# Hybrid trunk on one core: the product of a hi weight tile with the hi and lo halves of x becomes one of 512 columns, in strips 256 wide

## The chip, the cores and the metric

The kernel runs on one core of one Trainium2 chip. The metric is the device time of one execution in microseconds (us). The kernel before took 2446.97 us, the median of 3 runs (2446.15 to 2449.27).

## The reference, cut to what matters

One sequence of T = 256 tokens with D = 2048 features goes through two layers in float32. Each layer is a mixer and a dense SwiGLU, both between RMS norms:

```python
x = x + rms_norm(mixer(rms_norm(x, pre)), post)
x = x + rms_norm((silu(h @ w_gate) * (h @ w_up)) @ w_down, ffn_post)   # h = rms_norm(x, ffn_pre)
```

D_FF is 5632, so w_gate and w_up are 2048 x 5632 and w_down is 5632 x 2048. The mixer of the even layer is one input projection (2048 x 4384), an S5 state-space part, an RWKV-7 part and an output projection (2048 x 2048). The mixer of the odd layer is an input projection (2048 x 4096), a causal convolution over 4 tokens, gates from eight 256 x 256 blocks, a linear recurrence, and an output projection (2048 x 2048). All weights are float32 and are read once from memory, some 400 MB.

## The kernel before, in words

**Layout.** Features lie on the 128 partitions, tokens along the free axis. An activation is 16 tiles of 128 x 256 (one per 128 features, called a k tile where it is multiplied). A weight tile of 128 x 128 is the stationary operand, a tile of x the moving one, and the product, 128 output features x 256 tokens, adds up in PSUM over the k tiles.

**Hi and lo halves.** Float32 accuracy is kept with operands of type float32r: each operand z is split into hi, a rounded copy made on ScalarE, and lo = z - hi, made on VectorE (`split`, L288, through the helpers at L136 and L112). A weight tile times a tile of x is three products: hi with xh (L513), hi with xl (L514), lo with xh (L515), each of 256 columns, each with a weight load of its own. The text calls these three a triple.

**The weight stream.** Weights come in groups: one DMA of 512 KB, 2 k tiles by 512 output columns, into a tile `raw`; ScalarE writes `hi`, VectorE writes `lo`, in rings of 3 buffers (4 after the even layer). `plan` (L431) lists all groups in the order of use, `fetch` (L404) starts their DMAs, `ready` (L415) issues their splits three groups ahead of TensorE.

**Strips.** A `Strip` (L460) makes 512 output columns: four tiles of 128 features accumulate side by side in two PSUM banks (`psw0`, `psw1`, two of each), over all k tiles (`run`, L493). At its end (`done`, L535) an evac function reads PSUM: `first_evac` (L1477) copies on ScalarE, `last_evac` (L1483) adds to what lies in SBUF on VectorE, `gate` (L1658) multiplies by 1/rms of each token, applies silu, multiplies gate by up and splits the result into `hhi` and `hlo`. The last strip of a product finishes its PSUM banks one after the other (`tail`, L527).

**Stages.** Even layer: input strips w_u, w_lr and w_p, with S5 and RWKV work of many small float32 products between them, then w_glu and two halves of the output projection w_eo. SwiGLU: two halves, each of 11 gate-and-up strips and 4 down strips over 22 k tiles. Odd layer: 8 strips w_oi (256 columns of the gelu branch and 256 of the recurrent one), each but the first followed by a short strip w_gt of the gate blocks of the block before (2 k tiles), then 4 strips w_oo. Then the second SwiGLU. At the start of a stage `post` (L1579) makes the new x tile by tile, and the first strip follows it.

**Order.** Nothing is reordered at run time within an engine. What runs beside the weight stream is written as generators in lanes (`Lanes`), and the code issues their next step when an estimate of the engines' times says that its input is there. L.now, the estimate of TensorE's time, goes on by 0.327 for each triple. This decides only the order in which instructions stand on each engine.

## Time and profile before

| what | value |
|---|---|
| median of 3 runs | 2446.97 us |
| span of the profiled execution | 2446.8 us |
| TensorE matmul busy | 2373.5 us, 97% of the span |
| TensorE weight load busy | 2328.5 us, 95% |
| VectorE busy | 1469.4 us, 60% |
| ScalarE busy | 1181.0 us, 48% |
| GpSimd busy | 411.8 us, 17% |
| mean granted TensorE clock | 0.983 of full speed |
| read from memory | 397.98 MB, 164 GB/s over the span |

The trace holds one execution; its span from the first to the last instruction is 2446.8 us, so it and the median of the runs agree within 0.2 us. Matmuls are pipelined, and the end of each is modelled: a single one of 256 columns is shown as some 280 ns long, although the next one starts some 120 ns after it. So the length of a product is read here as the distance from its start to the start of the next, or as the length of a stretch divided by the number of products in it, and not as its mean duration. TensorE has two rows: PE for products, PEld for weight loads, which run while the product before streams. In order of time the stages are: even layer to 578 us, first SwiGLU to 1350 us, odd layer to 1663 us, second SwiGLU to the end.

### The profile page before, as it was taken

Reading aid. Unit: us, or ns where it says so; the run is one execution under the profiler, and the core shown is the slowest. Engines: PE = TensorE matmul, PEld = TensorE weight load, DVE = VectorE, ACT = ScalarE, POOL = GpSimd, SP = SyncE. Lnnn points to the kernel's source line nnn. Section 1 sums busy time; section 2 is a strip of 40 time slices with the busy share of each in tenths; the row PEclk is TensorE's granted clock in tenths of the full one; section 3 lists DMA queues with packets and bytes.
Section 4 is the critical chain, followed back from the end, with each engine's and each line's share of the span. In section 5 each row is a group of like instructions: output and inputs, shape, how many; then the busy total and the mean of one; then the engine's idle time right before and its main releaser. Section 6 shows DMA issues by size and latency. Waiting matters only on the chain.

```text
span 2446.8 us, 47370 instructions
## 1 busy us (share of the span) xinstructions
PE 2373.5 (97%) x19830; PEld 2328.5 (95%) x19830; DVE 1469.4 (60%) x2002; ACT 1181.0 (48%) x1550; POOL 411.8 (17%) x589
## 2 busy tenths in 40 slices
PE   7889999999999999999999999999999999999997
PEld 7888988998999999999999899998999999999997
DVE  8777667558655544555544877757555544555544
ACT  5547555545444434434433588845444444444443
POOL 4753666506000000000000400014000000000002
PEclk8888999999999999999999999999999999999999
DMA  5122543444555555555555455554555555555553
GB/s 198 58 71 73 156 123 113 143 141 164 186 185 182 185 186 184 182 186 183 183 187 181 139 181 188 175 197 138 183 185 186 182 187 183 183 186 183 182 186 116
DMA packets 127446, 404.21 MB, mean 165 GB/s; under 512 B 26112, under 2 KB 26880, under 8 KB 127104
## 3 DMA queue, kind: packets, MB, share of 16 engines
q1 hardware_dynamic: 126912, 399.61, 48.6%
q8 instruction: 155, 2.54, 0.4%
q0 software_dynamic: 320, 1.58, 0.2%
q14 instruction: 59, 0.48, 0.1%
HBM read 397.98 MB, written 3.15 MB: 164 GB/s over the span
## 4 chain that ended last, share of the span: by engine, by line
PE 73%; DVE 3%; POOL 1%; ACT 1%; issue 1%; POOLq 0%; ACTq 0%; DVEq 0%
PE psw L513 24%; PE psw L515 24%; PE psw L514 24%; DVE lo L112 1%; DVE xl L131 1%; POOL xr L112 1%; ACT hi L136 0%; PE ssq L263 0%; PE warm L263 0%; PE own L515 0%; PE own L514 0%; PE own L513 0%; POOL sqs L112 0%; DVE sqs L112 0%; POOL tg L112 0%
## 5 line engine op out<-in xcount | busy, mean ns | idle before, releaser
L112 DVE TENSOR_TENSOR lo<-raw,hi 128x1024 fp32r<-128x1024 f32 (+1 forms) x760 | 930.8, 1229 | 864.8 <-ACT hi L136 860.5
L136 ACT ACTIVATE hi<-raw 128x1024 fp32r<-128x1024 f32 (+1 forms) x760 | 783.7, 1035 | 938.6 <-PE psw L514 738.4
L514 PE MATMUL psw<-xl,hi 128*128 128x256 f32 x3328 | 942.2, 283 | 15.1 <-DVE xl L131 14.8
L513 PE MATMUL psw<-xh,hi 128*128 128x256 f32 x3328 | 941.4, 283 | 0.9 <-ACT xh L136 0.9
L515 PE MATMUL psw<-xh,lo 128*128 128x256 f32 x3328 | 940.3, 283 | 0.0
L514 PEld LDWEIGHTS psw<-xl,hi 128*128 128x128 f32 x3328 | 635.2, 191 | 19.8 <-DVE xl L131 19.8
L513 PEld LDWEIGHTS psw<-xh,hi 128*128 128x128 f32 x3328 | 635.3, 191 | 1.5 <-ACT xh L136 1.5
L515 PEld LDWEIGHTS psw<-xh,lo 128*128 128x128 f32 x3328 | 635.5, 191 | 0.0
L515 PE MATMUL psw<-hhi,lo 128*128 128x256 f32 x1364 | 384.4, 282 | 0.0
L513 PE MATMUL psw<-hhi,hi 128*128 128x256 f32 x1364 | 384.3, 282 | 0.0
L514 PE MATMUL psw<-hlo,hi 128*128 128x256 f32 x1364 | 383.8, 281 | 0.0
L112 POOL TENSOR_TENSOR sqs<-sqs 128x512 f32<-128x512 f32 x44 | 73.1, 1661 | 1518.8 <-ACT sqs L136 1518.4
L515 PEld LDWEIGHTS psw<-hhi,lo 128*128 128x128 f32 x1364 | 257.7, 189 | 0.0
L514 PEld LDWEIGHTS psw<-hlo,hi 128*128 128x128 f32 x1364 | 257.7, 189 | 0.0
L513 PEld LDWEIGHTS psw<-hhi,hi 128*128 128x128 f32 x1364 | 257.7, 189 | 0.0
L513 PE MATMUL psw<-hh,hi 128*128 128x256 f32 x560 | 175.8, 314 | 2.7 <-ACT hh L136 1.4
L514 PE MATMUL psw<-hl,hi 128*128 128x256 f32 x560 | 165.5, 296 | 5.3 <-DVE hl L131 5.3
L515 PE MATMUL psw<-hh,lo 128*128 128x256 f32 x560 | 165.6, 296 | 4.2 <-DVE lo L112 4.2
L513 PEld LDWEIGHTS psw<-hh,hi 128*128 128x128 f32 x560 | 112.8, 202 | 10.5 <-issue 5.6
L514 PEld LDWEIGHTS psw<-hl,hi 128*128 128x128 f32 x560 | 113.0, 202 | 6.2 <-DVE hl L131 5.9
L515 PEld LDWEIGHTS psw<-hh,lo 128*128 128x128 f32 x560 | 112.6, 201 | 5.8 <-DVE lo L112 5.6
L136 ACT ACTIVATE ga<-ga 128x512 f32<-128x512 f32 x52 | 32.9, 632 | 83.0 <-DVE ga L112 82.9
(426 smaller groups left out, 2760.6 us busy)
## 6 DMA issues: line engine op xcount, KB each, us to landing
raw<-in_w_fg SPq DMA_DIRECT2D x352, 512.0 KB, 3.5
raw<-in_w_fd SPq DMA_DIRECT2D x176, 512.0 KB, 3.5
raw<-in_w_oi SPq DMA_DIRECT2D x64, 512.0 KB, 3.9
raw<-in_w_p SPq DMA_DIRECT2D x64, 384.0 KB, 3.2
raw<-in_w_eo SPq DMA_DIRECT2D x32, 512.0 KB, 3.6
raw<-in_w_oo SPq DMA_DIRECT2D x32, 512.0 KB, 4.1
raw<-in_w_u SPq DMA_DIRECT2D x16, 512.0 KB, 4.0
raw<-in_w_glu SPq DMA_DIRECT2D x8, 512.0 KB, 3.5
```

Source lines behind the costliest of these rows:

```text
L112: e.tensor_tensor(o, x, y, op=op)
L131: e.scalar_tensor_tensor(o, x, s, y, op0=op0, op1=op1)
L136: S.activation(o, x, f, bias=bias, scale=scale)
L513: TE.matmul(o, hi[:, kk, sl], xh, start=st, stop=False, skip_group_check=True)
L514: TE.matmul(o, hi[:, kk, sl], xl, start=False, stop=False, skip_group_check=True)
L515: TE.matmul(o, lo[:, kk, sl], xh, start=False, stop=en, skip_group_check=True)
```

## The change

A tile of x now holds hi and lo next to each other (512 columns, class `Pair`; `hh` and `oh` likewise). One product of hi with both halves has 512 columns and fills one PSUM bank, its first half with hi times xh and its second with hi times xl; the product of lo with xh adds to the first half. A weight tile therefore takes two products and two weight loads instead of three. One output tile now takes a whole bank, so a strip is two tiles wide (256 columns, `W2`) and a group is 4 k tiles by 256 columns, the same 512 KB. The two halves in PSUM are added when they are read: ScalarE copies the second half of both tiles to SBUF, VectorE adds the first (`merged`, into a ring of two tiles `mo`). In `last_evac` VectorE adds both halves to SBUF itself, in two instructions.

What depends on the width moves along. `first_evac`, `gate` and the rest read the merged tile in SBUF. The gate strips of a SwiGLU hold one gate tile and one up tile; its halves are 24 and 20 such strips (`HF`) with 24 and 20 k tiles in the down products, 8 strips each. At a stage's start two strips run side by side (`two`), so that each new tile of x is still used by four output tiles. The odd layer has separate strips for the recurrent branch (`hawk_x`) and the gelu branch (`hawk_g`); the gate strips use four banks of their own (`own`). There ScalarE first writes the second half plus the bias to SBUF, VectorE adds the first half, and then the sigmoid runs over 512 columns; two products of 512 columns go from VectorE to GpSimd. L.now goes on by 0.335 for each pair. The diff, cut to its core:

```diff
+        class Pair:
+            def __init__(self, n, name):
+                self.s = [slot8(name=f"{name}{j}").rearrange("p (k z) t -> p k z t", z=2) for j in range(n // 4)]
...
+            def __call__(self, k):
+                return self.s[k // 4][:, k % 4]
...
-                self.ps = Banks(tail)
+                if own:
+                    self.ps = [bank("own").rearrange("p (z t) -> p z t", z=2) for _ in widths]
+                else:
+                    t = psw.tile([P, 2, 2, T], F32, tag="w", name="psw")
+                    self.ps = [t[:, j] for j in range(2)]
+                    self.both = t
...
-                        TE.matmul(o, hi[:, kk, sl], xh, start=st, stop=False, skip_group_check=True)
-                        TE.matmul(o, hi[:, kk, sl], xl, start=False, stop=False, skip_group_check=True)
-                        TE.matmul(o, lo[:, kk, sl], xh, start=False, stop=en, skip_group_check=True)
-                        L.now += 0.327
+                        TE.matmul(o, hi[:, kk, sl], x, start=k == 0, stop=False, skip_group_check=True)
+                        TE.matmul(o[:, 0], lo[:, kk, sl], x[:, 0], start=False, stop=en, skip_group_check=True)
+                        L.now += 0.335
...
+            def merged(self, o=None):
+                w, n = min(self.widths), len(self.widths)
+                if o is None:
+                    while len(held) > 1:
+                        L.step()
+                    o = mg.tile([P, 2, T], F32, tag="mo", bufs=2, name="mo")[0:w, 0:n]
+                    held.append(self)
+                act(o, self.both[0:w, 0:n, 1], AF.Copy)
+                tt(V, o, self.both[0:w, 0:n, 0], o, ADD)
+                return o
...
+        def two(a, b):
+            for g in range(a.kg - 1):
+                ta, tb = a.take(g), b.take(g)
+                for kk in range(0, a.kc, 2):
+                    for z, t in ((a, ta), (b, tb)):
+                        z.run(*t, kks=(kk, kk + 1))
+            for z in (a, b):
+                z.go(z.kg - 1)
...
             def first_evac(y, s):
-                def f(ps):
-                    for j in range(2):
-                        act(yv(y, s, j), ps[:, 2 * j:2 * j + 2], AF.Copy)
+                def f(z):
+                    z.merged(yv(y, s))
...
+                    if add:
+                        tt(V, o, z.both[:, n, 0], o, ADD)
+                        tt(V, o, z.both[:, n, 1], o, ADD)
+                    else:
+                        act(o, z.both[:, n, 1], AF.Copy)
+                        tt(V, o, z.both[:, n, 0], o, ADD)
...
+        def normed_later(z, rstd, rest):
+            o = z.merged()
+            def f():
+                while "rstd" not in rstd:
+                    yield 0.3
+                yield from after(rstd["rstd"])
+                tt(V, o, o, bc(rstd["rstd"], 1, 2), MUL)
+                yield from after(o)
+                yield from rest(o)
+            return f()
...
                 def gate(i):
+                    def rest(o):
+                        g = o[:, 0]
+                        act(g, g, AF.Silu)
+                        yield from after(g)
+                        tt(V, g, g, o[:, 1], MUL)
+                        yield from after(g)
+                        split(hh[:, i, 0], hh[:, i, 1], g)
+                        have.add(i)
+                    return lambda z: normed_later(z, rstd, rest)
...
             def gates(n):
-                        act(sr[:, j], pg[:, j], AF.Sigmoid, 1.0, vc("br", i))
-                        act(si[:, j], pg[:, 2 + j], AF.Sigmoid, 1.0, vc("bi", i))
+                    for o, q, b in ((sr, 0, "br"), (si, 2, "bi")):
+                        for j in range(2):
+                            act(o[:, j], z.ps[q + j][:, 1], AF.Identity, 1.0, vc(b, 2 * n + j))
+                    for o, q in ((sr, 0), (si, 2)):
+                        for j in range(2):
+                            tt(V, o[:, j], z.ps[q + j][:, 0], o[:, j], ADD)
+                            rel(z.ps[q + j])
...
+                        for o in (sr, si):
+                            yield from after(o)
+                            act(o, o, AF.Sigmoid)
...
-                        tt(V, si, si, xc, MUL)
+                        tt(G, si, si, xc, MUL)
```

On TensorE, in the down products of the SwiGLU, the kernel before issues three products of 256 columns for each of the four output tiles (`hhi` and `hlo` are the halves of the moving operand, `psw0` and `psw1` the two banks):

```order
L513 MATMUL psw1_14691<-hhi_11263,hi_14756 128x256
L514 MATMUL psw1_14691<-hlo_11264,hi_14756 128x256
L515 MATMUL psw1_14691<-hhi_11263,lo_14757 128x256
...
L513 MATMUL psw0_14690<-hhi_11263,hi_14756 128x256
L514 MATMUL psw0_14690<-hlo_11264,hi_14756 128x256
L515 MATMUL psw0_14690<-hhi_11263,lo_14757 128x256
```

The changed kernel issues two there, at the end of one strip and the start of the next:

```order
L515 MATMUL psw_8563<-hh_6075,hi_8611 128x512
L516 MATMUL psw_8563<-hh_6075,lo_8612 128x256
L515 MATMUL psw_8563<-hh_6075,hi_8611 128x512
L516 MATMUL psw_8563<-hh_6075,lo_8612 128x256
L515 MATMUL psw_8703<-hh_6075,hi_8635 128x512
L516 MATMUL psw_8703<-hh_6075,lo_8636 128x256
```

Each weight tile has one product and one weight load less, and a strip's PSUM is full after half as many of them as before.

On VectorE, in a gate-and-up stage, this is what one strip of 512 columns puts between the splits of the weight stream (`lo<-raw,hi`) before:

```order
L112 TENSOR_TENSOR ga_8167<-psw0_7922,rstd_7453 128x512
L112 TENSOR_TENSOR ub_8168<-psw1_7923,rstd_7453 128x512
L112 TENSOR_TENSOR lo_8175<-raw_8051,hi_8174 128x1024
L112 TENSOR_TENSOR ga_8167<-ga_8167,ub_8168 128x512
L112 TENSOR_TENSOR lo_8206<-raw_8081,hi_8205 128x1024
L112 TENSOR_TENSOR hlo_7006<-ga_8167,hhi_7005 128x512
L112 TENSOR_TENSOR lo_8238<-raw_8111,hi_8237 128x1024
```

And this is what a strip of 256 columns puts there now (`mo` is the merged tile):

```order
L112 TENSOR_TENSOR lo_10105<-raw_10011,hi_10104 128x1024
L112 TENSOR_TENSOR mo_10126<-psw_10032,mo_10126 128x512
L112 TENSOR_TENSOR lo_10131<-raw_10037,hi_10130 128x1024
L112 TENSOR_TENSOR mo_10126<-mo_10126,rstd_6437 128x512
L112 TENSOR_TENSOR lo_10154<-raw_10060,hi_10153 128x1024
L112 TENSOR_TENSOR mo_10126<-mo_10126 128x256
L112 TENSOR_TENSOR lo_10178<-raw_10084,hi_10177 128x1024
L112 TENSOR_TENSOR hh_9648<-mo_10126,hh_9648 128x256
```

The add of the halves has come in ahead of the multiplication by 1/rms, once for every 256 output columns; the two last steps work on half as many columns.

On ScalarE, in the odd layer, the gates of one block of 256 features (`sr`, `si`) and what follows them stand so before:

```order
L136 ACTIVATE sr_16080<-psw0_16046,vec_79 128x256
L136 ACTIVATE si_16081<-psw1_16047,vec_79 128x256
...
L136 ACTIVATE hi_16090<-raw_15949 128x1024
L136 ACT_TABLE_LOAD
L136 ACTIVATE av_16082<-sr_16080,m8_6963 128x256
L136 ACTIVATE sr_16080<-sr_16080,p8_6964 128x256
...
L136 ACTIVATE a2_16083<-av_16082 128x512
```

and so now:

```order
L136 ACTIVATE si_14124<-own_14095,vec_82 128x256
L136 ACTIVATE si_14124<-own_14096,vec_82 128x256
...
L136 ACT_TABLE_LOAD
L136 ACTIVATE sr_14123<-sr_14123 128x512
L136 ACTIVATE si_14124<-si_14124 128x512
L136 ACT_TABLE_LOAD
L136 ACTIVATE av_14125<-sr_14123,m8_6033 128x256
...
L136 ACTIVATE ga_14225<-mo_14090 128x512
L136 ACTIVATE mo_14239<-psw_14135 128x512
```

The four reads of PSUM stay, the two sigmoids over 512 columns come after them, behind an add on VectorE, and each of the two strips of a block now ends with a copy of PSUM to `mo`.

## Rows read from the trace of the kernel before

**Rows 1.** The page, parts 1 and 4: busy us and count; the chain's shares.
```profile
PE 2373.5 (97%) x19830; PEld 2328.5 (95%) x19830; DVE 1469.4 (60%) x2002; ACT 1181.0 (48%) x1550; POOL 411.8 (17%) x589
...
PE 73%; DVE 3%; POOL 1%; ACT 1%; issue 1%; POOLq 0%; ACTq 0%; DVEq 0%
```

**Rows 2.** Windows: length, busy (count) of PE, PEld, DVE, ACT, POOL; clock; DMA.
```profile
0.00:250.00 250.00, 213.16 (x1521) 200.79 (x1522) 198.80 (x416) 140.20 (x257) 133.66 (x173) 0.85 0.30 100
250.00:578.00 328.00, 323.44 (x2983) 297.72 (x2981) 211.94 (x423) 166.50 (x288) 158.99 (x320) 1.00 0.46 142
845.00:965.00 120.00, 120.00 (x1011) 120.00 (x1011) 52.31 (x44) 47.91 (x49) 0.00 (x0) 1.00 0.55 187
970.00:1215.00 245.00, 245.00 (x2051) 245.00 (x2050) 130.60 (x126) 100.51 (x106) 0.00 (x0) 1.00 0.54 185
1411.00:1514.00 103.00, 103.00 (x865) 103.00 (x865) 78.48 (x100) 85.08 (x112) 0.42 (x4) 1.00 0.55 185
```

**Rows 3.** Windows of L513 alone, one product of each triple: PE and PEld only.
```profile
0.00:2446.80 2446.80, 1700.40 (x5936) 1135.47 (x5936) 0.98 0.49 165
250.00:578.00 328.00, 175.64 (x581) 110.38 (x581) 1.00 0.46 142
...
1350.30:1563.50 213.20, 160.63 (x568) 108.13 (x568) 1.00 0.52 176
```

**Rows 4.** Timeline of PE near 101 us: start us, us, what.
```profile
100.86 0.28 PE L513 MATMUL psw<-hh,hi 128*32 128x256 f32 x1
100.98 0.28 PE L514 MATMUL psw<-hl,hi 128*32 128x256 f32 x1
101.10 0.28 PE L515 MATMUL psw<-hh,lo 128*32 128x256 f32 x1
101.22 0.28 PE L513 MATMUL psw<-hh,hi 128*128 128x256 f32 x1
```

**Rows 5.** Timeline of PEld in the same stretch.
```profile
100.63 0.19 PEld L515 LDWEIGHTS psw<-hh,lo 128*128 128x128 f32 x1
100.75 0.11 PEld L513 LDWEIGHTS psw<-hh,hi 128*32 128x32 f32 x1
100.87 0.11 PEld L514 LDWEIGHTS psw<-hl,hi 128*32 128x32 f32 x1
```

**Rows 6.** Windows, all engines, near the start: the clock is the first share.
```profile
10.00:16.00 6.00, 4.52 (x21) 4.52 (x22) 6.00 (x16) 4.01 (x8) 1.50 (x1) 0.50 0.94 376
```

**Rows 7.** Timeline of PE in that stretch.
```profile
12.08 0.41 PE L513 MATMUL psw<-hh,hi 128*128 128x256 f32 x1
12.29 0.41 PE L514 MATMUL psw<-hl,hi 128*128 128x256 f32 x1
12.50 0.41 PE L515 MATMUL psw<-hh,lo 128*128 128x256 f32 x1
```

**Rows 8.** Groups of ACT by shape: xcount | busy us, mean ns | idle before.
```profile
L136 ACT ACTIVATE ga<-ga 128x512 f32<-128x512 f32 x52 | 32.9, 632 | 83.0 <-DVE ga L112 82.9
...
L136 ACT ACTIVATE ya<-psw 128x512 f32<-128x512 f32 x12 | 7.2, 598 | 10.9 <-PE psw L515 10.2
```

**Rows 9.** Groups of DVE by shape.
```profile
L112 DVE TENSOR_TENSOR ya<-psw,ya 128x512 f32<-128x512 f32 x12 | 8.2, 690 | 0.1
...
L112 DVE TENSOR_TENSOR yb<-psw,yb 128x256 f32<-128x256 f32 x3 | 1.3, 425 | 1.8 <-PE psw L515 1.8
```

**Rows 10.** Groups of ACT by shape from 1411 to 1514 us.
```profile
L136 ACT ACTIVATE hi<-raw 128x1024 fp32r<-128x1024 f32 x36 | 37.2, 1054 | 17.2 <-PE psw L514 17.2
L136 ACT ACT_TABLE_LOAD x16 | 20.5, 1283 | 0.3
```

**Rows 11.** The chain of waits from 1350 to 1376 us: start us, us, what.
```profile
1364.00 1.70 POOL xr L112
1365.69 1.43 POOL sqs L112
1367.98 1.70 POOL xr L112
```

More of the change, by code (lines that the diff above doesn't have):

```diff
@@ L708, in gamma @@
                 def gamma():
-                    g = [tiny() for _ in range(4)]
+                    g = room[14:18]
                     nr = r1
@@ L1152, in solve @@
                 H = HV[hf]
-                while "ready" not in H:
+                while "ready" not in H or hf > 1 and hf - 2 not in cdone:
                     yield 0.5
@@ L1468, in build, with glu_split @@
-            for s in range(2):
-                strip(w_glu[s], of1(ygs), W4, glu_evac(s))
+            def glu_split():
+                while "p" not in R2:
+                    yield 0.3
+                ygs.append(Pair(8, "yg"))
+                for k in range(0, 8, 2):
+                    ygs[0].split(k, 2, ygt[0][:, k:k + 2])
+                    yield 2.0
+            stbd = []
+            for j in range(12):
+                if j == 11:
+                    L.add("gs", glu_split())
+                strip(w_p[j], hx, W2, elem(j))
@@ new lines, in rest @@
+                def rest(o):
+                    sq = ssq.place()
+                    act(sq, o, AF.Square)
+                    yield from after(sq)
+                    ssq.pair(sq, V if s == 6 else G)
+                    for i in range(2):
+                        scaled(2 * s + i)
+                    if s == 6:
+                        yield from ssq.flush()
+                return f
+            for s in range(8):
+                strip(w_eo[0][s], ysp, W2, first_evac(y, s))
+            yr = Pair(8, "yr")
@@ L1679, in ffn @@
+                for i in range(n):
+                    if hf or i > 1:
+                        strip(w[i], x, W2, gate(i))
+                    elif i == 0:
+                        two(Strip(w[0], x, W2, gate(0), mid=mid), Strip(w[1], x, W2, gate(1)))
                 if hf == 0:
```

759 lines of the change are left out of this document (363 added, 396 removed).

## The prediction

> **What bounds the kernel now.** I read the page first: TensorE is busy 97% of the span, and the chain of work that ended last runs over it for 73% [rows 1]. Then the windows by stage, where the reader is to compare the engines with each other: in the SwiGLU TensorE has no idle time at all (120.00 of 120.00 us in a down stage, 245.00 of 245.00 in a gate-and-up stage), while VectorE and ScalarE are busy 40 to 53% [rows 2]. So the stream of products sets the time there, and the question is what a product costs. In the down stage 1011 products take 120.00 us, 118.7 ns each; in the gate-and-up stage 2051 take 245.00 us, 119.5 ns [rows 2]. A triple is 356 or 358 ns. There are 5936 of them [rows 3], so triples make up 5936 x 357 ns = 2119 us of the 2446.8.
>
> Third, what a product of 256 columns would need by itself. Near the start the granted clock was at its lower level, 0.50 of 2.4 GHz [rows 6], and there the starts are 0.21 us apart [rows 7]: 256 columns at 1.2 GHz are 213 ns, one column per period and nothing on top. At 2.4 GHz the columns alone are 106.7 ns, so the full clock shows an excess of 12.0 ns per product in the down stage and 12.8 in the gate-and-up stage. The change turns on where this excess comes from.
>
> Fourth, whether it is the weight load. In the even layer one tile has 32 output features: its loads show as 0.11 us instead of 0.19 [rows 5], and its products still start 0.12 us apart [rows 4]. A load a quarter as wide leaves the distance, so I put the excess on the product, once for each.
>
> **One product of 512 columns for two of 256.** No product of this width and type is in the trace. From below it costs its columns, 213.3 ns; from above two of today's products, 238 ns. I take 213.3 plus one excess, 225.7 ns, the value that rows 4 to 7 lie nearest to. The product of lo stays at 119. A triple of 357.4 becomes a pair of 345.0, and 12.4 ns are saved (bounds: nothing and 24.8).
>
> *SwiGLU and w_oo.* Gate and up have 2 x 1408 triples. At a stage's start the x tiles come from a chain on GpSimd, two tiles every 4 us (1364.00 to 1367.98) [rows 11], about as fast as the first strip uses them; `two` keeps four output tiles for each x tile, so those 64 triples per layer gain nothing. (2816 - 128) x 12.8 ns = 34.4 us. Down: 2 x 704 x 12.0 = 16.9 us. w_oo: 256 x 12.0 = 3.1 us. Together 54.4 us.
>
> *Even layer.* From 250 us on TensorE is busy 323.44 of 328 us at the full clock [rows 2], with 581 triples in it [rows 3]: 581 x 12.4 = 7.2 us. Of the 299 before 250 us I count none: the mean clock is 0.85 [rows 2], at the half clock there is no excess to save, and TensorE is idle 37 us for want of input (bound: 3.7 us).
>
> *w_oi of the odd layer.* From 1411 to 1514 us there are four blocks of 25.75 us, and ScalarE is busy 85.08 us of it [rows 2], 21.3 per block, of which weight splits and table loads are two thirds; it idles only for buffers that TensorE has to give back [rows 10]. The change adds per block two copies out of PSUM at 0.598 and two sigmoids over 512 columns, by the row of silu over 512 at 0.632 [rows 8], while the four reads of PSUM stay: 23.8 us. TensorE would need 72 pairs x 345 = 24.8 us. That leaves ScalarE one microsecond for all its waits for VectorE, of which two per block are new, and the splits stand behind those waits in its queue. I take it that ScalarE keeps the block at its 25.75 us: no gain. Bounds: the whole gain of 568 x 12.4 = 7 us [rows 3], or a loss of 1.5 us per block, 12 us.
>
> **What is added and hidden.** Every strip of 256 columns ends with a copy (0.598) and an add (0.690) [rows 8, 9] before its two banks are free. The strip that needs them starts one strip later, 32 x 345 ns = 11 us, so in the SwiGLU TensorE hides the 1.3 us; there ScalarE and VectorE each get about 1.3 us more work per 22 us and have over 10 us to spare. If nothing hid it, the 120 SwiGLU strips would cost 156 us. Behind the copy in ScalarE's queue stand splits of groups that TensorE needs two groups later, 5.5 us on; behind the add in VectorE's stand the same groups. In the even layer 22 strips are merged; there ScalarE is busy 51% and VectorE 65% from 250 us on [rows 2], TensorE hides it again, and the bound without cover is 22 x 1.29 = 28 us. The weight DMAs move the same bytes in the same 512 KB pieces at a share of 0.55 [rows 2] and have room for 4% more. The two products of 512 moved to GpSimd fall where it is idle (0.42 of 103 us) [rows 2].
>
> At the ends of w_eo, w_oo and both down products the reading of the last bank lies on the path: one more instruction over 256 columns, 0.425 [rows 9], four times, 1.7 us.
>
> **Sum.** 54.4 + 7.2 - 1.7 = 59.9 us off the profiled 2446.8: 2386.9. The median of the runs is 0.2 us above the span, so 2387.
>
> **Rivals.** *The excess is the load's (2325 us).* Load and product are about equally long and follow each other without a gap, PEld being busy 95% [rows 1]; perhaps each short product waits for a load, and a product twice as long covers it. Then 512 columns take 213.3, the pair 332.4, and a triple saves 25 ns: (2688 + 1408 + 256) x 25 = 108.8, the even layer 14.5, less 1.7, w_oi bounded by ScalarE as before: 2446.8 - 121.6 = 2325. Rows 4 and 5 speak against it, for three products only. The Trainium skill (TensorE: Matmul & The Clock Gate, section Back-to-back issue gap) says that in a stream of load and matmul the spacing is set by both together; for the 32-column loads here the trace does not bear this out.
>
> *The excess goes with the columns (2457 us, slower).* The moving operand of four bytes per value may come a ninth too slowly at the full clock, which the half clock would not show either. Then 512 columns take 238 ns, the pair 357, TensorE saves nothing, and what was added decides: 1.7 us at the ends and, in the even layer, where VectorE is busy 65 to 80% and the lanes wait for each other, a third of the 28 us: 2446.8 + 11 = 2457. It decides once a product of 512 columns starts more than about 236 ns before the next. For it: the excess differs with the stage although the products are alike, 12.0 against 12.8. Against it: a rate exact to a ninth needs a cause that no row shows. The Trainium skill (TensorE: Matmul & The Clock Gate, section Wait — 56ns, not 53.3ns?) puts the fixed part of a warm matmul at 2.5 ns; of the 12.4 only that would be saved, an estimate of some 12 us on 4933 triples, which would end a little below today's time. The 118.7 ns here are not its 109, so the trace differs from it in size; whether in kind, no row before the change shows.
>
> *Crowding (2408 us).* TensorE saves as forecast, but ScalarE and VectorE, which are in order and wait for each other, give part of it back where they are full: in w_oi 14 us (27.5 us per block), in the even layer the 7.2. 2387 + 21 = 2408. For it: ScalarE's 23.8 of 24.8 us. Against it: today ScalarE waits only for TensorE there [rows 10].
>
> **How the numbers follow.** Forecast 0.49 (its own range 2372 to 2400), the load's excess 0.20, crowding 0.18, columns 0.13. 0.2% is about what a measurement of this kernel tells from no change: 2442 to 2452 is the same. Slower holds most of the columns' case, 0.10; the same is what is left of it and the worst of the crowding, 0.05; faster 0.85. The range takes in the load's case and the crowding, 2318 to 2440, and leaves out the columns' case and the edges.
>
> **What would show it.** The start of a product of 512 columns stands 0.226 us before the next one, that of 256 columns 0.119, also where the clock is full. If 0.214, the load was the cause; if 0.238, the columns. A down stage of 704 pairs over both halves takes 243 us instead of 251; a gate-and-up window still shows TensorE busy throughout, with VectorE and ScalarE below 70%. The w_oi stage stays at 213 us with ScalarE above 88% and, new, waits of ScalarE for VectorE rather than for TensorE. Idle time of TensorE before the first product of a strip would show that the merge is not hidden. The forecast is wrong if the pair is not between 0.340 and 0.350 us, or if the even layer, 578 us long today, moves by more than 15 us.

## The result and the profile after

The changed kernel takes 2505.48 us (median of 4 runs, 2496.48 to 2508.24) beside 2446.97 us of the kernel before on the same chip (median of 3 runs; a fourth took 3222.87 us and is left out as a slow one). By the means it takes 1.0231 times as long, 95% interval 1.0211 to 1.0251. The forecast was 2387 us; the change costs some 57 us where 60 were to be gained.

The first lines of the page, busy time by engine and the chain that ended last:

```profile
PE 2366.4 (94%) x13894; PEld 2046.1 (82%) x13894; DVE 1585.3 (63%) x2259; ACT 1271.3 (51%) x1771; POOL 423.3 (17%) x604
...
PE 71%; DVE 3%; ACT 2%; POOL 1%; issue 1%; POOLq 0%; DVEq 0%; ACTq 0%
```

Against [rows 1] TensorE has 30% fewer products, hardly less busy time, and a longer span. Where it went shows by stage (from the first product of a stage to the first of the next, profiled executions):

| stage | before, us | after, us | |
|---|---|---|---|
| even layer | 578.0 | 633.6 | +55.6 |
| first SwiGLU | 772.3 | 760.8 | -11.5 |
| w_oi | 213.2 | 217.9 | +4.7 |
| w_oo with the last gate strip | 99.9 | 124.2 | +24.3 |
| second SwiGLU | 783.4 | 769.9 | -13.5 |

The even layer of the seven profiled kernels with the same program up to there (this one, e_oo, e_oo2, e_oo3, e_lane, e_lane3 and e_noadd_oi below) lies between 624 and 634 us, so its loss is 46 to 56 us, and differences of under 10 us in it say little. The windows that answer to [rows 2] (length; busy time and count of PE, PEld, DVE, ACT, POOL; granted clock; DMA share; GB/s) are the start, the rest of the even layer, a down stage, a gate-and-up stage and w_oi:

```profile
0.00:250.00 250.00, 208.58 (x1159) 178.87 (x1160) 196.91 (x393) 142.03 (x245) 131.46 (x162) 0.80 0.30 99
250.00:633.00 383.00, 349.38 (x2459) 287.60 (x2458) 239.07 (x462) 183.12 (x304) 156.48 (x331) 0.91 0.40 123
920.00:1040.00 120.00, 120.00 (x685) 104.87 (x684) 57.87 (x51) 48.59 (x51) 0.00 (x0) 1.00 0.58 189
1060.00:1260.00 200.00, 200.00 (x1151) 175.91 (x1150) 123.61 (x144) 96.07 (x126) 0.00 (x0) 1.00 0.58 190
1450.00:1553.00 103.00, 103.00 (x591) 90.25 (x590) 87.55 (x115) 94.06 (x129) 13.72 (x11) 1.00 0.58 189
```

**The SwiGLU.** TensorE has no idle time there, as forecast, and the merges lie under the products. In the down stage 685 products take 120.00 us, 350.4 ns per pair. The starts show how it divides:

```profile
1099.81 0.39 PE L515 MATMUL psw<-x,hi 128*128 128x512 f32 x1
1100.04 0.28 PE L516 MATMUL psw<-x,lo 128*128 128x256 f32 x1
1100.15 0.39 PE L515 MATMUL psw<-x,hi 128*128 128x512 f32 x1
1100.38 0.28 PE L516 MATMUL psw<-x,lo 128*128 128x256 f32 x1
```

The product of 512 columns starts 0.23 us before the next, that of 256 columns 0.11 to 0.12. Over whole stages a pair is 348.9 ns (223.3 us for 640 in gate-and-up) or 351.4 (134.9 for 384 in down), where a triple was 359.3 or 356.7: 5 to 10 ns less, not 12.4. At the starts and ends of the stages some of this is lost again, as e_three below shows. In the even layer, at the lower clock level (1.2 GHz), a product of 512 columns starts 427 ns before the next (the median), one column per period, as [rows 7] have it for 256.

**The even layer from 250 us on.** The kernel before idles 4.6 us there at the full clock [rows 2]. Now TensorE idles 383.00 - 349.38 = 33.6 us and the mean clock is 0.91; by the granted clock of each stretch 57 us of its busy time lie at the lower level (1.2 of 2.4 GHz), work that takes 28 us at the higher. 29 us more of idle time and 28 lost to the half clock are what the layer is longer by. Its waits, between 250 and 633 us (in all, times, longest):

```profile
PE bp L280 <- DVE av L131: 12.6, 3, 7.9
PE tp L287 <- DVE yc L112: 5.6, 2, 4.2
PE psw L515 <- DVE yb L112: 2.8, 1, 2.8
PE wa L280 <- DVE bv L112: 2.4, 1, 2.4
```

`bp` and `wa` belong to the preparation of a head pair of the RWKV, `tp` to its norm. The wait for `yb` is the only longer one for an add of halves. The two tiles of a strip now lie in one PSUM tile, and at the end of the last strip the second tile's products wait until VectorE has added the two halves of the first:

```profile
624.77 0.88 DVE L112 TENSOR_TENSOR yb<-psw,yb 128x256 f32<-128x256 f32 x2
```

The same wait stands at the ends of w_oo and of the two SwiGLUs, with 1.3, 1.7 and 1.0 us; the kernel before has none of the four. The longest wait, followed back over three timelines, VectorE, POOL and TensorE:

```profile
440.49 0.41 DVE L120 TENSOR_SCALAR av<-av,hka,oka 128x256 f32<-128x256 f32 x1
449.99 0.51 DVE L131 SCALAR_TENSOR_TENSOR av<-rk,vec 128x256 f32<-128x256 f32 x1 [9.08 <-POOL rk L112]
```

```profile
430.74 0.24 POOL L112 TENSOR_TENSOR sq<-lf,lm 128x31 f32<-128x31 f32 x1 [10.75 <-DMA lm<-mtd]
...
448.92 0.31 POOL L112 TENSOR_TENSOR lf<-lf,sq 128x60 f32<-128x60 f32 x1
449.17 0.11 POOL L160 MEMSET pp<- 128x4 f32 x1
449.22 0.73 POOL L112 TENSOR_TENSOR rk<-rk,av 128x256 f32<-128x256 f32 x1
```

```profile
450.64 0.77 PE L280 MATMUL bp<-av,cst 128*128 128x256 f32 x1 [7.88 <-DVE av L131]
```

`rk` is k times av, 0.73 us of work. Its input is ready at 441, but it stands on POOL behind 18 us of the solve of a head group (`lf`, `sq`), which itself waited for a DMA. VectorE waits for it, with the weight splits behind in its queue, and TensorE waits for VectorE. Then the clock falls (the same stretch after and before):

```profile
447.00:465.00 18.00, 11.96 (x38) 7.92 (x38) 9.55 (x20) 5.31 (x9) 12.55 (x33) 0.53 0.16 58
```

```profile
447.00:465.00 18.00, 17.87 (x160) 15.94 (x159) 9.84 (x16) 8.35 (x14) 15.18 (x37) 1.00 0.37 128
```

**w_oo.** The kernel before has no wait of TensorE over 0.2 us from 1540 to 1663. Now, from 1390 to 1740 us:

```profile
PE psw L515 <- DVE oh L112: 9.9, 1, 9.9
PE psw L515 <- DVE x L131: 7.8, 5, 2.4
PE own L515 <- DVE xs L112: 7.1, 1, 7.1
PE ssq L280 <- DVE sr L112: 5.3, 1, 5.3
```

`xs` is the input of the last gate strip, `oh` the output of the gates that w_oo multiplies; `x` is the start of a stage, as before. `sr` is the add of a gate strip's halves, after which its PSUM banks are free. A gate strip now holds all four banks that the small products share, and the sum of squares `ssq`, which needs one of them, waits 5.3 us for the last strip's. In w_oi itself, in the last of the windows above, TensorE is busy throughout (103.00 of 103.00), with ScalarE at 94.06. From the first product of a gate strip to that of the next pass 25.06 to 25.30 us (five blocks from 1450.8 to 1576.5), before 25.75 to 25.80.

### The profile page after: what moved, and what is told of

Its sections match the earlier page's. It is cut to its first block, busy times and chain, and to the rows that moved or that the text cites. A ratio compares the mean times of both kernels' runs of the same rounds, so it can differ in the third digit from the quotient of the medians.

```text
span 2506.5 us, 35871 instructions
## 1 busy us (share of the span) xinstructions
PE 2366.4 (94%) x13894; PEld 2046.1 (82%) x13894; DVE 1585.3 (63%) x2259; ACT 1271.3 (51%) x1771; POOL 423.3 (17%) x604
## 4 chain that ended last, share of the span: by engine, by line
PE 71%; DVE 3%; ACT 2%; POOL 1%; issue 1%; POOLq 0%; DVEq 0%; ACTq 0%
PE psw L515 46%; PE psw L516 24%; DVE lo L112 1%; DVE x L131 1%; ACT hi L136 1%; ACT L136 0%; PE own L515 0%; POOL xr L112 0%; PE warm L280 0%; PE ssq L280 0%; ACT sr L136 0%; DVE yb L112 0%; ACT x L136 0%; PE own L516 0%; ACT sqs L136 0%
## 5 line engine op out<-in xcount | busy, mean ns | idle before, releaser
L112 DVE TENSOR_TENSOR lo<-raw,hi 128x1024 fp32r<-128x1024 f32 x741 | 924.6, 1250 | 588.3 <-ACT hi L136 587.0
L515 PE MATMUL psw<-x,hi 128*128 128x512 f32 x3328 | 1169.9, 395 | 22.1 <-DVE x L131 21.7
L136 ACT ACTIVATE hi<-raw 128x1024 fp32r<-128x1024 f32 x741 | 781.7, 1057 | 697.0 <-PE psw L515 353.4
L516 PE MATMUL psw<-x,lo 128*128 128x256 f32 x3328 | 935.7, 281 | 0.3 <-DVE lo L112 0.3
L515 PEld LDWEIGHTS psw<-x,hi 128*128 128x128 f32 x3328 | 625.6, 188 | 170.5 <-DVE x L131 29.1
L516 PEld LDWEIGHTS psw<-x,lo 128*128 128x128 f32 x3328 | 630.1, 189 | 0.7 <-DVE lo L112 0.7
L515 PE MATMUL psw<-hh,hi 128*128 128x512 f32 x1408 | 495.6, 395 | 2.6 <-DVE yb L112 2.6
L516 PE MATMUL psw<-hh,lo 128*128 128x256 f32 x1408 | 397.1, 282 | 0.0
L515 PE MATMUL psw<-h,hi 128*128 128x512 f32 (+1 forms) x560 | 233.3, 449 | 8.8 <-DVE h L131 8.5
L516 PE MATMUL psw<-h,lo 128*128 128x256 f32 (+1 forms) x560 | 168.3, 301 | 3.3 <-DVE lo L112 3.3
```

The source lines that it names most:

```text
L112: e.tensor_tensor(o, x, y, op=op)
L136: S.activation(o, x, f, bias=bias, scale=scale)
L515: TE.matmul(o, hi[:, kk, sl], x, start=k == 0, stop=False, skip_group_check=True)
L516: TE.matmul(o[:, 0], lo[:, kk, sl], x[:, 0], start=False, stop=en, skip_group_check=True)
```

## The experiments

Ratios are to the kernel before, which ran beside each (medians 2446.1 to 2448.8 us), with 95% intervals. Two theories ran through them. A: the product saves some 7.5 ns wherever TensorE is the bound, and the rest is lost where chains of small steps (RWKV, gates) stand in the order of issue and have fewer products over them. Against it: the wide product, or the work of adding the halves, makes the loss.

**The product alone.**

```diff
-TE.matmul(o, hi[:, kk, sl], x, start=k == 0, ...)
+TE.matmul(o[:, 0], hi[:, kk, sl], x[:, 0], start=k == 0, ...)
+TE.matmul(o[:, 1], hi[:, kk, sl], x[:, 1], start=False, ...)
```

> The kernel after with the product of 512 columns taken apart into two of 256 (three products per weight tile again, everything else, the strips of 256, the halves of PSUM added on reading and the order of emission, as in the kernel after). Theory A: the wide product itself saves only some 7.5 ns per weight tile (348.9 to 351.4 ns against 356.7 to 359.3 in the steady stages of the two traces), and the even layer is longer because of the chain of the RWKV and of the strips around it, not because of the product. Then the SwiGLUs get longer by about 4224 x 7.5 ns = 32 us in all, the u, p and w_oi stages by some 8 us more, and the even layer as a whole moves by less than 8 us: 2535 to 2550 us. Rival B: it is the wide product that holds TensorE up (a bank of PSUM written over all its columns, a wait for it somewhere), so that three narrow ones give back most of the 58 us: 2450 to 2480 us.

2542.81 us, 1.0392 [1.0369, 1.0415]. A down stage and a gate-and-up stage:

```profile
920.00:1040.00 120.00, 120.00 (x1012) 120.00 (x1011) 56.88 (x51) 47.93 (x49) 0.00 (x0) 1.00 0.60 185
1060.00:1260.00 200.00, 200.00 (x1675) 200.00 (x1675) 119.56 (x141) 93.59 (x123) 0.00 (x0) 1.00 0.59 183
```

118.6 and 119.4 ns per product, as in [rows 2]; the stages are back at 356.7 and 359.3 ns per triple to the tenth. The even layer is 624.6 us, no longer than with wide products. So the wide product gains, and the even layer's length does not hang on it. The two SwiGLUs take 777.2 and 786.6 us, 16.4 and 16.7 more than in the kernel after, but also 4.8 and 3.2 more than in the kernel before, with triples as long as there: the strips of 256 columns themselves cost 8 us at the starts and ends of these stages.

**The change in the SwiGLUs alone.** The kernel before, with the new strips and products in `ffn` and `post`, each output tile in a PSUM tile of its own; even and odd layer as before:

```diff
-                    strip(w_fg[l][11 * hf + i], x, W4, ...
+                        strip2(w[i], x, W2, gate(i))
```

> The kernel before with the change in its two SwiGLUs alone: strips of 256, products of 512 and 256 columns there, an output to a bank, halves added by an instruction for each output; even and odd layer as before. Theory A (the product saves 7 to 8 ns per weight tile wherever TensorE is the bound, and everything that the change lost it lost in the even layer and w_oo): the SwiGLUs get shorter by 11.5 and 13.5 us as they did in the kernel after: 2417 to 2428 us, faster than both kernels. Rival (the shorter SwiGLU of the kernel after owes its gain to something else of that kernel, such as the longer pauses ahead of it): 2440 to 2450 us, the same as before.

2422.83 us (2418.59 to 2427.08), 0.9904 [0.9888, 0.9920]: faster than both kernels, in the middle of what was expected. A gate-and-up and a down stage of it:

```profile
700.00:830.00 130.00, 130.00 (x749) 114.27 (x748) 81.13 (x106) 63.77 (x93) 0.00 (x0) 1.00 0.58 188
845.00:965.00 120.00, 120.00 (x686) 104.97 (x685) 61.08 (x67) 51.85 (x63) 0.00 (x0) 1.00 0.57 186
```

**What the excess belongs to.** The lo product made with the hi weights, and the lo product as two of 128 columns:

```diff
-TE.matmul(o[:, 0], lo[:, kk, sl], x[:, 0], ...)
+TE.matmul(o[:, 0], hi[:, kk, sl], x[:, 0], ...)
```

```diff
+for c in (slice(0, P), slice(P, T)):
+    TE.matmul(o[:, 0, c], lo[:, kk, sl], x[:, 0, c], ...)
```

> The kernel after, with the narrow product also made with the hi weight tile in place of the lo one (the lo halves are still made, what they would give is left out of the results), so that both products of a pair have the same weights. Asks where the 29 to 31 ns of a pair above its 768 columns come from. Rival theory of the prediction (a change of weights costs it): the pair falls by 10 ns or more, the kernel by 4224 x 10 = 42 us or more, below 2465 us. Theory A (it belongs to the product, a fixed part of some 7 ns and a part with its columns, whatever the weights): pairs stay at 349 to 351 ns: 2495 to 2508 us.

> The kernel after with the lo product as two products of 128 columns in place of one of 256 (four per weight tile pair in place of three, the same columns in all). Read from the steady stretch of the SwiGLU alone. Theory A (a product costs its columns at 2.4 GHz, some 6.9 ns, and some 2 per cent of its columns' time on top: 117 to 120 ns at 256, 224 to 234 at 512): one more product adds some 7 ns to each pair, 349 to 356. Rival (12 ns for each product, whatever its columns, as the prediction had it): 361. Time in all: 2535 us by the one, 2555 by the other.

With equal weights: 2500.48 us, 1.0218 [1.0202, 1.0234], pairs of 348.9 and 351.4 ns as in the kernel after. That the weights differ costs nothing of its own; each product still has its load there (13894 of either), so this says nothing on the load. With 128 columns: 3062.22 us in a single run, and both theories are far off. TensorE's products and loads there:

```profile
1519.80 0.45 PE L515 MATMUL psw<-hh,hi 128*128 128x512 f32 x1
1520.09 0.33 PE L517 MATMUL psw<-hh,lo 128*128 128x128 f32 x2
1520.25 0.45 PE L515 MATMUL psw<-hh,hi 128*128 128x512 f32 x1
```

```profile
1520.20 0.19 PEld L515 LDWEIGHTS psw<-hh,hi 128*128 128x128 f32 x1
1520.31 0.42 PEld L517 LDWEIGHTS psw<-hh,lo 128*128 128x128 f32 x2
1520.65 0.19 PEld L515 LDWEIGHTS psw<-hh,hi 128*128 128x128 f32 x1
```

From one hi product to the next 0.45 us pass in place of 0.35: the columns are the same, so one more product with its load costs 0.10. Two loads that follow each other without a wide product stand 0.11 us apart (1520.20, 1520.31). This fits a load that takes 0.11 us and can't be hidden under 128 columns, which need 0.053; under 256 columns (0.107) it nearly can, and those products start 0.117 to 0.120 apart. The Trainium skill (TensorE: Matmul & The Clock Gate, section LDWEIGHTS (loading the stationary operand)) gives a load a time in ns of its columns divided by 1.2, an estimate of 107 ns for 128 columns. The 0.11 us of the trace agree with it. What the 0.017 us of a 512-column product above its columns are stays open.

**The adds of the halves.** Out everywhere but in the last strips of a product, where VectorE copies the first half instead (e_nomerge; the code is simplified), and then in w_oi alone, where the next instruction reads the first half from PSUM (e_noadd_oi):

```diff
-act(o, self.both[0:w, 0:n, 1], AF.Copy)
-tt(V, o, self.both[0:w, 0:n, 0], o, ADD)
+V.tensor_copy(o, self.both[0:w, 0:n, 0])
```

> The kernel after, in which the reading of PSUM that adds the halves is left out: no ScalarE copy of the second half, and VectorE copies the first half where it added the two (so what x lo times the weights gives is left out of the results; the last strips of w_eo, w_fd and w_oo, which add both halves to y, stay as they are). Order of emission unchanged. About 598 ns of ScalarE and some 100 to 300 ns of VectorE go from each such strip. Theory A (the even layer is held up by the order, the run-ahead in PSUM and the chain of RWKV): the even layer gets shorter by less than 10 us, the SwiGLUs, whose merges lie under the products, by less than 2 us: 2494 to 2506 us. Rival C (the merges crowd VectorE and ScalarE, and the chain of RWKV waits for them): the even layer loses 20 us or more, and w_oi, where VectorE is at 82 and ScalarE at 84 per cent, some 4 us: 2465 to 2485 us.

2496.37 us, 1.0199 [1.0182, 1.0217]. The even layer is 623.8 us, at the edge of the 624 to 634 of those with the adds, and w_oi and w_oo take 342 us as in the kernel after.

> The kernel after, in which the 16 strips of w_oi aren't added from halves: the next instruction reads the first half of PSUM where it read the sum (what x lo times the weights gives is left out there), so that each strip has 598 ns of ScalarE and 690 of VectorE less, 9.6 and 11 us together. Two changes of order left w_oi and w_oo as long as they were (342 us in the kernel after; 340 and 342). Theory A (in w_oi VectorE and ScalarE, at 84 and 82 per cent, set the pace of a head's chain, and the merges are what put them behind; the kernel before has 313 us there at 78 and 77 per cent): the two stages get shorter by 15 us or more: 2475 to 2490 us. Rival (the latency of one head's chain from its x strip to oh and the 48 pairs that are left over it, whatever the engines have beside it): less than 8 us: 2497 to 2506 us.

2507.31 us, 1.0237 [1.0219, 1.0254]; w_oi and w_oo take 348 us, and TensorE waits 8.3 us for `xs` and 10.1 for `oh`. In the window that answers to w_oi above VectorE is down from 87.55 us to 78.53:

```profile
1450.00:1553.00 103.00, 98.56 (x561) 85.61 (x561) 78.53 (x99) 87.39 (x117) 11.75 (x11) 1.00 0.56 177
```

TensorE is no longer busy throughout, and a block takes 26.9 to 27.0 us: PSUM is now read later, and TensorE waits 5.9 us for ScalarE's reading of it (`ga`). So this run is not a clean test, but e_nomerge, with blocks of 25.1 to 25.3 us and 342 us for both stages, is. The work of adding the halves is not what was lost, in either layer, but for the waits at the ends of the stages, where both runs leave the adds in. The theory that VectorE and ScalarE set the pace of w_oi falls.

**The order of issue in the RWKV.** One instruction per head pair, then all four, from POOL to VectorE:

```diff
-tt(G, k, k, av, MUL)
+V.tensor_tensor(k, k, av, op=MUL)
```

> The kernel after with one instruction of each of the eight head pairs of the RWKV on VectorE where it was on POOL (k times av, 128x256). In the kernel after this one stands on POOL behind some 18 us of the solve of a head group, VectorE idles 9.5 us for it and TensorE 8.3 for what VectorE makes next (av), at 428 us, and 17 to 20 us of half clock follow. Theory A (such a block of the engines in their order of issue makes a good part of what the even layer lost: 29 us of idle TensorE and 28 us of half clock from 248 us on, where the kernel before has 4.6 and none): that wait goes, and the even layer gets shorter by 8 to 18 us: 2482 to 2493 us. Rival (the chain of the RWKV has its length from its DMAs and its solve, and the last outputs come no earlier when TensorE waits less before): 2497 to 2506 us.

(The 428 us of this text are the place in the profile of e_oo; in the kernel after it is 440 to 450.) 2488.06 us, 1.0164 [1.0149, 1.0179], the whole gain in the even layer, 610.6 us. The 12.6 us for `av` are gone; the next block shows:

```profile
PE wa L280 <- DVE bv L112: 8.0, 1, 8.0
PE tp L287 <- DVE yc L112: 5.6, 2, 4.2
```

> As e_rk, with the other three POOL instructions of a head pair of the RWKV on VectorE too (a memset of pp, and the second halves of bk and ar). In e_rk the wait at 428 us went, but VectorE idles 3.4 us for that memset behind the next solve on POOL, ScalarE 5.2 us for VectorE and TensorE 8.0 us (wa for bv), and 10 us of half clock follow. Theory A (such blocks in the order of issue are what lengthens the even layer): that wait goes too, 8 to 16 us off e_rk: 2472 to 2481 us. Rival (what is left of the loss is the length of the chain itself, whichever engine has these instructions): 2483 to 2490 us, as e_rk.

2486.20 us, 1.0156 [1.0138, 1.0174], even layer 609.8: the wait of 8.0 for `bv` gives way to one of 4.1 for `sw`, and nothing is gained. The rival holds for the second step. Why shows in three moments of the RWKV (us; first `qp` of the first solve, last `gp`, end of the layer):

| | first qp | last gp | end | chain | rest |
|---|---|---|---|---|---|
| before | 248 | 541 | 578 | 293 | 37 |
| after | 265 | 582 | 634 | 317 | 52 |
| e_rk | 262 | 557 | 611 | 295 | 53 |
| e_rk2 | 262 | 554 | 610 | 292 | 56 |

The chain is back at the length it had; what is left is its start, 14 us later, and the rest behind it.

> The kernel after with the planner's margin, after which an instruction that depends on another engine is issued, at 1.5 us in place of 0.5; this moves the issue of the RWKV's and S5's steps later by a microsecond each and changes nothing else. Theory A (the even layer loses its time where engines are blocked by what was issued too early by the planner's unchanged prices, not by the work that is there): fewer and shorter waits of TensorE from 248 us on (33.7 us now) and less half clock: 2485 to 2500 us. Rival (the RWKV's chain is the bound, and a microsecond on each of its steps makes it longer): 2510 to 2540 us.

(`MARGIN = 1.5` in place of 0.5.) 2536.54 us, 1.0360 [1.0343, 1.0376], even layer 649.7: the rival. Issuing later doesn't help; the chain starts at 284.

**The run-ahead, and the gate of the solve.** The gate is a line of the change that has not been named so far: the solve of a head group waits, in the order of issue, for the chunks of the group two before it. Both in the kernel before:

```diff
-e0 = eo(0).go(*range(3))
-e1 = eo(1).go(*range(3))
+e0 = eo(0).go(0)
+e1 = eo(1).go(0)
```

```diff
-while "ready" not in H:
+while "ready" not in H or hf > 1 and hf - 2 not in cdone:
```

> The kernel before, in which the first two strips of the second half of w_eo run ahead of the last outputs of the RWKV by one group each in place of three: 16 triples, as many as the pairs that the kernel after has there with its 512 columns of PSUM in flight, in place of 48. Nothing else is changed. Theory A (the run-ahead that PSUM allows covers the end of the chain of the RWKV): 32 triples of 357 ns, 11 us, come out from under it; TensorE waits there in place of 1.4 us up to some 11, with some half clock behind it: 2452 to 2465 us. Rival (in the kernel before the chain ends so early that 16 triples do, and what the even layer lost comes from the chain's own delay alone): 2445 to 2450 us.

2456.33 us, 1.0033 [1.0021, 1.0046], and the layer 585.8 us. TensorE waits 4.2 us for `yc`, which it did not do before, and the rest behind the chain is 50 us in place of 37, as in the kernel after.

> The kernel before with one line of the change alone: the solve of head group 2 (3) isn't begun before the chunks of group 0 (1) are issued. In the kernel before these chunks end at 360 and 420 us and those solves begin at 361 and 426, so Theory A expects no more than 2 us: 2445 to 2450 us. Rival (the gate itself pushes the solves and all that follows back by 10 us or more): 2456 us and more.

2450.15 us, 1.0007 [0.9997, 1.0017]: no effect in the kernel before, whose chunks end as those solves begin. In the kernel after, the solves of groups 2 and 3 begin at 404.9 and 495.6 us, each 1.8 us behind the end of those chunks (403.1, 493.8); what the gate does there was not tried.

**The end of w_oi and w_oo.** Three orders of the strips, and two lanes in place of one. The first lines are no code but the order of issue from there on; `x`, `g` and `gt` are the strips of a head:

```diff
-x6 g6 gt5 x7 gt6 g7 gt7 oo
+x6 gt5 x7 gt6 g6 gt7 g7 oo               # e_oo
+x5 gt4 x6 g5 x7 gt5 g6 gt6 g7 gt7 oo     # e_oo2
+x7 g5 gt5 g6 gt6 gt7 g7 oo, x two ahead  # e_oo3
-... gates(n), lane="hg", ...
+... gates(n), lane=f"hg{n % 2}", ...     # e_lane, e_lane3
```

> The kernel after with another order at the end of w_oi alone: both x strips of the last two heads come first, the gate strip of head 7 before the last g strip instead of behind it, so that 64 more pairs of products lie over the chain from the last gate to the last two tiles of oh. In the kernel after TensorE idles 24.6 us in w_oo with its last gates, 9.9 of them for oh, 7.1 for xs and 5.3 for sr. Theory A (too few products are left to cover that chain): 10 to 20 us shorter there, nothing elsewhere: 2485 to 2496 us. Rival (the chain is behind because VectorE and ScalarE are, at 82 and 84 per cent busy in w_oi): less than 5 us: 2500 to 2508 us.

> The kernel after with the order of w_oi changed from head 5 on: x5 gt4 x6 g5 x7 gt5 g6 gt6 g7 gt7 and then w_oo, so that between the end of an x strip and its gate strip 48 to 56 pairs of products lie (17 to 20 us), and 104 pairs between x7 and the last groups of w_oo. Where e_oo moved the gates forward, TensorE only waited earlier for xs (8.5 and 4.5 us) and the two stages together got shorter by 2 us. Theory A (from an x strip to its xs some 15 us pass, from a gate strip to oh some 27, and every product that lies between covers a part of it): the waits of w_oi and w_oo, 32 us together in the kernel after, fall to some 15, with the half clock that follows them: 2483 to 2493 us. Rival (VectorE and ScalarE are behind by their own work in w_oi, and where products lie makes no difference): as e_oo, 2496 to 2506 us.

> The kernel after with the x strips of w_oi two heads ahead of the g strips (x0 x1 x2 g0 gt0 x3 g1 gt1 ... x7 g5 gt5 g6 gt6 gt7 g7, then w_oo); xs is kept in the part of oh that its head fills later, which makes room for two more buffers of xc. 48 pairs then lie between x7 and its gate strip, and 64 behind that, where the kernel after has 24 and 48. Theory A (from an x strip to xs pass some 15 us and from a gate strip to oh some 27, by the waits seen with 24 and 48 pairs, and only the products that lie between cover them, however much work VectorE has beside): the wait for xs goes, that for oh falls from 9.9 us to 5 or less, and w_oi and w_oo get shorter by 12 to 22 us with the half clock: 2480 to 2492 us. Rival (e_oo, e_oo2 and e_noadd_oi left the two stages at 340 to 348 us because something else sets their end): 2496 us and more.

e_oo: 2499.08 us, 1.0220 [1.0201, 1.0239], w_oi and w_oo 340 us together (342 in the kernel after). e_oo2: 2502.44, 1.0224 [1.0204, 1.0244], 342 us. e_oo3: 2496.96, 1.0205 [1.0180, 1.0230], 339 us. Theory A failed in this form three times. The longest waits of e_oo and of e_oo3:

```profile
PE own L515 <- DVE xs L112: 13.0, 2, 8.5
...
PE psw L515 <- DVE oh L112: 6.5, 1, 6.5
```

```profile
PE psw L515 <- DVE oh L112: 10.1, 1, 10.1
...
PE own L515 <- DVE sr L112: 5.7, 1, 5.7
```

More products behind the last gate strip leave the wait for `oh` at 10: the trace counts 84 pairs up to that wait in e_oo3 and 52 in the kernel after (the 64 and 48 of the texts are too few). What stood in the way shows on ScalarE in the kernel after (durations, then first and last start):

```profile
L136 ACT ACTIVATE sr<-own,vec x2: 456/460/464, 1622.1 to 1622.5; 128x256 f32<-128x256 f32 x2
L136 ACT ACTIVATE sr<-sr x2: 631/632/633, 1631.3 to 1640.3; 128x512 f32<-128x512 f32 x2
```

Gate strip 7 is read at 1622, and its sigmoid (the second `sr<-sr`) begins at 1640.3, when head 6 has its `oh`: both stand in one lane. From the reading of a gate strip to its `oh` 42 and 32 us pass for the last two heads, before 21 and 19.

> The kernel after with one word changed: what follows a gate strip is issued in one of two lanes by turns of the heads, and no longer in one lane, in which a head's chain begins only when the one before it has ended. In the kernel after 42 us pass from the reading of gate strip 6 (1598.5) to oh of head 6 (1640.3) and 32 for head 7 (1622.1 to 1654.3), in the kernel before 21 and 19 us, and the sigmoid of head 7 begins at 1640.3, when head 6 is through. Theory A (the chains of the last two heads, made longer by the added halves and run one behind the other, set the end of w_oo, and where the products lie changes only what covers them): the wait for oh (9.9 us) goes down by 6 us or more and w_oi and w_oo together from 342 to 322 to 334 us: 2484 to 2497 us. Rival (ScalarE and VectorE run the two chains in the same time however they are issued): within 4 us, 2497 us and more.

> e_oo3 with the two lanes of e_lane. e_oo3 took away the wait for xs (7.1 us), but one for sr (5.7) came in its place and that for oh stayed at 10.1 us, with 64 pairs behind the last gate strip. Theory A (the chains one behind the other are what was left): both waits go down, w_oi and w_oo from 339 to 315 to 328 us: 2473 to 2488 us. Rival: as e_oo3, 2491 us and more.

e_lane: 2493.30 us, 1.0186 [1.0170, 1.0201], w_oi and w_oo 333.6 us. e_lane3: 2487.21, 1.0151 [1.0129, 1.0173], 328.8 us. The waits of e_lane:

```profile
PE own L515 <- DVE xs L112: 15.7, 1, 15.7
...
PE psw L515 <- DVE oh L112: 1.7, 1, 1.7
```

With two lanes the wait for `oh` falls to 1.7 us; that for `xs` grows, and the order of e_oo3 takes that one away too. In e_lane3 neither is left. It takes both: 13 of the 29 us that the two stages had lost are back. The longest single wait that e_lane3 still has there is

```profile
PE own L515 <- DVE sr L112: 5.0, 1, 5.0
```

Gate strip 7 waits there until the adds of strip 6 have freed the four banks. Banks of its own for each were not tried.

> e_rk2 and e_oo3 in one kernel. Theory A (the two losses lie in different stages and don't touch): the sum of both gains, 2486 less what e_oo3 saves over the kernel after, 2462 to 2474 us, still slower than before (2447), since the later start of the RWKV's chain and the shorter run-ahead behind it stay. Rival: one gain takes the other's place, 2478 us and more.

2481.72 us, 1.0143 [1.0127, 1.0158], in the rival's range: 4.5 us below e_rk2, where e_oo3 saves 8.5 over the kernel after. But its stages are 611.0 and 339 us, those of e_rk2 and e_oo3, so by stage both gains are there, and the sum misses by the spread of these runs (e_oo3: 2490.53 to 2500.58).

## Why the prediction was wrong

**The product of 512 columns: mechanism right, size off.** "213.3 plus one excess, 225.7 ns": measured 230. The pair came out at 348.9 to 351.4 and not at 345.0, in part outside the 340 to 350 that the forecast set itself. So a triple saves 5 to 10 ns, some 8 on average, between the forecast and the rival in which the excess goes with the columns. The SwiGLUs give 25 us (11.5 and 13.5; 23.4 in the kernel with the change there alone) of the 51 counted for them. On the forecast's counts the measured pairs would give 35 us, an estimate from 10.4 and 5.3 ns; the other 10 go at the starts and ends of the stages. The 1.7 us counted for the ends were 6.8 us in waits for `yb` alone (2.8, 1.7, 1.3 and 1.0). The rival of the load (2325 us) would have had 0.213 us between the starts. By the fixed 2.5 ns per warm matmul of the Trainium skill (TensorE: Matmul & The Clock Gate, section Wait — 56ns, not 53.3ns?) 512 columns would take 215.8 ns, an estimate. The 230 here do not agree with it for operands of type float32r.

**The even layer: the step that failed.** "From 250 us on TensorE is busy 323.44 of 328 us ... 581 x 12.4 = 7.2 us", and for what is added "TensorE hides it again". TensorE was the bound there, but with the RWKV just under it: its last output came 37 us before the end of the layer, and three groups of two strips in flight were all that lay over it. I counted the merges as the threat, and nearly all of them cost little (e_nomerge; it takes out the 22 strips of the forecast's bound and also the 8 of the first half of w_eo, which the bound forgot). The change moved three other things that I left out. The solves stand at other places on POOL (some 17 us with the half clock behind them, e_rk). 512 output columns in flight instead of 1024, in groups of 4 k tiles instead of 2, leave 16 pairs of run-ahead for 48 triples (8 us in the kernel before, b_ahead). And the chain starts 10 to 18 us later (257.8 to 265.3 us in the seven kernels, 247.7 before). Added up this is 35 to 43 of the 46 to 56 us, an estimate; the rest stays open. The late start was not tried; the trace shows TensorE's first product at 11.5 us and not 7.8, since two strips start together, a u stage of 99.1 us for 92.2, and the first head pair complete after two strips of w_p and not one.

**w_oo: the second step that failed.** "w_oo: 256 x 12.0 = 3.1 us" was read as SwiGLU-like. It follows the gates, whose chain from reading to `oh` grew from 19 to 32 us for the last head and runs one head behind the other, with 52 pairs over it, some 18 us, where the kernel before had 64 triples, 23 us. +24.3 us; e_lane and e_lane3 show that the one lane and the cover are two of the causes. That the chain is also longer by the add before the sigmoid and the two products on POOL is argued, not shown. Of the loss of w_oi and w_oo, 29 us, 16 are left in e_lane3 and stay open; 5.0 us of waiting for the gate strips' banks is in them.

**w_oi** (no gain; bounds 7 us less, 12 more) moved by +4.7 us, within its bounds, but by luck. ScalarE is as full as forecast (91%), but the block is 25.1 us and not 25.75, with TensorE busy all the time: TensorE sets it, as it did before (with triples in e_three it is 25.75 to 25.80 again), and leaving the copies out did not shorten it (e_nomerge). The loss comes at the ends of the stage, 7.1 us of it the wait for `xs`. **Crowding** (2408 us) is refuted by e_nomerge: the loss is in queues behind waiting instructions, not in busy engines. The forecast named its own test, the even layer moving by more than 15 us; it moved by 46 to 56. The slower case was worked out for the wrong cause.

## What to carry to other kernels

Where a stage shows TensorE busy at 98%, look also at when the chain beside it ends and how many products are left then: the kernel stays bound by products only as long as those cover the chain. A change of tile width changes how much work can run ahead in PSUM and where every small instruction stands in its queue, and both can cost more than the product saves. Put such a change first where nothing else runs: in the SwiGLUs alone it gives 1.0%.

## What was not expected of the hardware

A float32r product of 512 columns starts 230 ns before the next at the full clock, 17 above its columns, and 427 at the half clock, nothing above them. Two products of 128 columns in place of one of 256, each with its load, make a pair 0.10 us longer (0.45 for 0.35 us), and the loads between follow each other 0.11 us apart. A wait of 7.9 us ended at 450.6 us, and from 447 to 465 us TensorE was at the lower clock level nearly throughout (0.53 on the mean). Its 11.3 busy us at that level are work of 5.7 at the higher, so that the wait cost some 1.7 times its length, an estimate.
